# A two-by-two block product of seven instead of eight in the up projection of the second layer, with its down projection in groups of four

## The chip, the cores and the metric

The kernel runs on one core of one Trainium2 chip. The metric is the device time of one execution in microseconds (us). A core has five engines with instruction streams of their own, each worked off in order: TensorE (PE, with its weight loads shown as PEld), VectorE (DVE), ScalarE (ACT), GpSimd (POOL) and SyncE (SP), which here issues the transfers. A wait of an instruction holds up all that stands behind it on its engine.

## What is computed

The reference is one inference step of a two-layer backbone with D = 1024 over 128 context and 512 latent tokens. A layer has a mixer (two kinds of attention and a Fourier mixing), then a gated feed-forward part with a convolution of width three over the tokens. The change concerns the second layer's feed-forward part alone:

```python
h = _modulate(x_l, g_ffn_norm[l], sf, cf)
x_l = x_l + gf * _conv_ffn(h, w_up[l], w_conv[l], w_down[l])

def _conv_ffn(h, w_up_l, w_conv_l, w_down_l):
    u = h @ w_up_l                      # 1024 -> 2 * 2816
    up = jnp.pad(u, ((0, 0), (1, 1), (0, 0)))
    u = sum(up[:, j:j + N] * w_conv_l[j] for j in range(3))
    gate, val = jnp.split(u, 2, axis=-1)
    return (jax.nn.silu(gate) * val) @ w_down_l   # 2816 -> 1024
```

Context and latent tokens take their own modulation and the same weights. At the end comes a norm of both streams.

## The kernel before

Features lie on the partitions and tokens on the columns: 642 columns, of which two are spare, in two halves of 322 and 320. For the convolution each half is taken with a column more on either side, so an up product has 324 columns.

Products have nearly the precision of fp32. Every operand is split (`hi_lo`, L111 to L113): ScalarE copies it rounded to `hi`, and VectorE or GpSimd subtracts to get `lo`. `mm3` (L130 to L133) then issues three matmuls, hi by hi, hi by lo and lo by hi. A weight tile is loaded by a transfer into `raw` and split into `whi` and `wlo` (`weight`, L119 to L125); the feed-forward part has two tiles of each, and a third of its own (`weight3`, L898).

The feed-forward part (`ffn`, L888 to L1032) first does the output projection of the mixer in two passes, one for each half, 8 output tiles each, with residual and squares. After a pass `stats` (L221 to L241) makes the norm of that half and `modulate` (L244 to L262) writes the modulated tiles `hh`, `hl` for eight feature tiles.

Then come 22 tiles j of hidden features, in groups of 8, 8 and 6 (`FGROUPS`, L38). For each j, L972 to L988 take a gate tile and a value tile: a weight tile of 128x1024, and for each half of the columns 8 steps of the contraction by three matmuls, so 96 matmuls of 324 columns per j, in a PSUM bank per product. ScalarE makes the middle tap (L983), VectorE the outer two (L984, L986), straight from PSUM. ScalarE makes the silu (L989), GpSimd multiplies (L990), ScalarE casts to `gh`, and GpSimd subtracts for `gl` (L993). Behind each group, L1001 to L1029 do its share of the down projection: for each of eight output tiles m and each half three matmuls per j, then the residual on VectorE (L859), in two pieces for the first half and one for the second. The last group does so in two passes, one per half, each with squares, the norm, and the scaled output tiles `y` (L1025), sent by SyncE.

PSUM has six banks for these products. The order on each engine is set by a scheduler that simulates a timeline when the kernel is built; the code's order and the number of buffers bound it.

## Time and profile before

| what | value |
|---|---|
| times of three runs | 1838.87, 1839.2, 1846.52 us |
| median | 1839.2 us |
| span of the profiled execution | 1843.6 us |
| TensorE busy | 1717.2 us, 93% |
| VectorE busy | 1166.4 us, 63% |
| ScalarE busy | 779.4 us, 42% |
| GpSimd busy | 650.0 us, 35% |

The profile is of one execution, whose span is listed beside the times; all durations come from it. In it the second layer's up and down projections take from about 1345 us to 1828 us, and the end of the output about 16 us more. Busy time of TensorE's matmuls is modelled, and neighbours overlap in the rows: the pace of matmuls is read from their number in a stretch without waits.

### The profile page before, as it was taken

The numbers are of one execution on the slowest core, as the hardware profiler recorded it, in microseconds if no ns is written. First come the engines' busy times: TensorE is split into PE (matmuls) and PEld (weight loads), VectorE is DVE, ScalarE is ACT, GpSimd is POOL, SyncE is SP. The second block draws the span as 40 slices with busy tenths as digits, with TensorE's granted clock in tenths as the row PEclk, the third lists the DMA queues.
The fourth block names the chain that finished last, engine by engine and source line by source line (L and its number), as shares of the span: only waits on it lengthen the run. The fifth ranks groups of instructions, "written<-read, shape, count | busy, mean of one in ns | idle before, by whom it ended". The sixth has DMA issues, their size and how long they took to land. (4 is left out here: it accounts for less than half of the span.)

```text
span 1843.6 us, 29032 instructions
## 1 busy us (share of the span) xinstructions
PE 1717.2 (93%) x11160; PEld 1670.1 (91%) x11160; DVE 1166.4 (63%) x2051; ACT 779.4 (42%) x1494; POOL 650.0 (35%) x719
## 2 busy tenths in 40 slices
PE   6988899986999999999999798999999999999997
PEld 5878899876899999999998787998999999999997
DVE  7628765679799999734455388865544434443445
ACT  5436564643543123313343466765433313321332
POOL 6547454548422112201242576562212201220222
PEclk9889898988899999999999899999999999999998
DMA  7367654655255565322254576562312222222223
GB/s 279 96 210 208 193 172 149 207 175 171 82 182 172 183 202 164 111 73 73 63 169 135 177 214 183 176 205 73 103 35 74 76 72 78 70 81 69 78 69 118
DMA packets 81084, 249.70 MB, mean 135 GB/s; under 512 B 10417, under 2 KB 19761, under 8 KB 79281
## 3 DMA queue, kind: packets, MB, share of 16 engines
q1 hardware_dynamic: 74226, 209.13, 35.6%
q0 software_dynamic: 6720, 38.72, 7.6%
q8 instruction: 88, 1.44, 0.3%
q14 instruction: 50, 0.41, 0.1%
HBM read 203.43 MB, written 41.24 MB: 133 GB/s over the span
## 5 line engine op out<-in xcount | busy, mean ns | idle before, releaser
L132 PE MATMUL up<-hl_o,whi 128*128 128x324 f32 x1408 | 441.2, 314 | 2.7 <-POOL hl_o L113 2.7
L131 PE MATMUL up<-hh_o,whi 128*128 128x324 f32 x1408 | 440.4, 314 | 2.3 <-ACT hh_o L260 1.2
L133 PE MATMUL up<-hh_o,wlo 128*128 128x324 f32 x1408 | 440.8, 314 | 0.0
L112 ACT CAST whi<-raw 128x1024 fp32r<-128x1024 f32 (+2 forms) x210 | 207.0, 989 | 434.7 <-PE dn L132 204.7
L113 DVE TENSOR_TENSOR wlo<-raw,whi 128x1024 fp32r<-128x1024 f32 (+2 forms) x184 | 227.0, 1237 | 203.4 <-ACT whi L112 199.2
L990 POOL TENSOR_TENSOR cg<-cg,cv 128x644 f32<-128x644 f32 x44 | 73.2, 1664 | 665.4 <-DVE cv L986 653.9
L132 PEld LDWEIGHTS up<-hl_o,whi 128*128 128x128 f32 x1408 | 268.0, 190 | 4.4 <-POOL hl_o L113 4.3
L131 PEld LDWEIGHTS up<-hh_o,whi 128*128 128x128 f32 x1408 | 267.8, 191 | 3.0 <-ACT hh_o L112 1.6
L133 PEld LDWEIGHTS up<-hh_o,wlo 128*128 128x128 f32 x1408 | 267.1, 190 | 0.0
L131 PE MATMUL dn<-gh,whi 128*128 128x322 f32 x704 | 218.7, 314 | 5.0 <-ACT gh L112 3.9
L132 PE MATMUL dn<-gl,whi 128*128 128x322 f32 x704 | 220.1, 313 | 0.0
L133 PE MATMUL dn<-gh,wlo 128*128 128x322 f32 x704 | 218.9, 313 | 0.0
L149 DVE CUSTOM_DVE_ANT_0 junk<-ada,scond 128x1024 bf16<-128x1024 f32 x138 | 199.4, 1445 | 4.4 <-ACT scond L143 2.8
L477 DVE TENSOR_REDUCE nm<-sc 128x1 f32<-128x640 f32 (+1 forms) x180 | 126.5, 711 | 76.5 <-PE sc L576 56.2
L478 ACT ACTIVATE P<-sc,nm 128x640 f32<-128x640 f32 (+1 forms) x180 | 128.1, 713 | 74.9 <-DVE nm L477 56.6
L859 DVE SCALAR_TENSOR_TENSOR x_x<-dn,mods,x_x 128x128 f32<-128x128 f32 (+2 forms) x144 | 57.6, 436 | 132.8 <-PE dn L133 132.7
L131 PEld LDWEIGHTS dn<-gh,whi 128*128 128x128 f32 x704 | 133.4, 190 | 6.9 <-ACT gh L112 4.1
L133 PEld LDWEIGHTS dn<-gh,wlo 128*128 128x128 f32 x704 | 133.8, 190 | 0.4 <-DVE wlo L113 0.4
L132 PEld LDWEIGHTS dn<-gl,whi 128*128 128x128 f32 x704 | 133.9, 190 | 0.3 <-POOL gl L113 0.2
L131 PE MATMUL proj<-hh_n,whi 128*128 128x320 f32 (+1 forms) x320 | 109.0, 341 | 5.7 <-ACT whi L112 3.0
L133 PE MATMUL proj<-hh_n,wlo 128*128 128x320 f32 (+1 forms) x320 | 106.8, 334 | 0.0
L132 PE MATMUL proj<-hl_n,whi 128*128 128x320 f32 (+1 forms) x320 | 106.5, 333 | 0.0
(299 smaller groups left out, 3740.0 us busy)
## 6 DMA issues: line engine op xcount, KB each, us to landing
raw<-in_w_up SPq DMA_DIRECT2D x88, 512.0 KB, 3.6
...
```

The costliest lines, as they stand in the source:

```text
L112: nc.scalar.copy(out=hi, in_=src)
L113: (lo_eng or nc.vector).tensor_tensor(out=lo, in0=src, in1=hi.bitcast(F32), op=ALU.subtract)
L131: nc.tensor.matmul(out, lhsT=lh, rhs=rh, start=first, stop=False)
L132: nc.tensor.matmul(out, lhsT=lh, rhs=rl, start=False, stop=False)
L133: nc.tensor.matmul(out, lhsT=ll, rhs=rh, start=False, stop=last)
L149: nc.vector.tensor_tensor_reduce(out=junk, in0=wt, in1=scond[:, c], op0=ALU.mult, op1=ALU.add, scale=1.0, scalar=0.0, accum_out=mods[:, l, ...
L477: nc.vector.tensor_reduce(out=nm, in_=s_in, axis=ax, op=ALU.max, negate=True)
L478: nc.scalar.activation(out=p_out, in_=s_in, func=AF.Exp, bias=nm, scale=1.0, accum_out=s_out)
L859: nc.vector.scalar_tensor_tensor(out=x[:, o:o + w], in0=ps, scalar=gate, in1=x[:, o:o + w], op0=ALU.mult, op1=ALU.add)
L990: nc.gpsimd.tensor_tensor(out=c[0], in0=c[0], in1=c[1], op=ALU.mult)
```

## The change

In the second layer (`SEVEN`) a tile j's gate and value weights are seen as a two-by-two block matrix (gate and value by two halves of the contraction, each 128x512: wa, wb for the gate, wc, wd for the value), and the tokens as another (two halves of the contraction by two halves of the columns: b11, b12, b21, b22). Their product is made from seven block products, numbered in the code:

| product | weight | tokens | goes to |
|---|---|---|---|
| 1 | wa | b11 | bank A, copied to s1 |
| 2 | wb | b21 | bank A on top: gate, first half |
| 6 | x6 = wc + wd + wa | -(b22 - b12) - b11 | bank B; u2 = B + s1 |
| 7 | wc + wa | b22 - b12 | bank B on top; u3 = B + s1, then C + u3: value, second half |
| 4 | wd | (b22 - b12) + b11 - b21 | bank B on top; + s1: value, first half |
| 5 | x5 = wc + wd | b11 - b12 | bank C |
| 3 | wb + x6 | b22 | bank C on top; + u2: gate, second half |

The signs of the value tile are turned, and its convolution's weights with them. The token blocks are combined once, behind the norm (`modulate32` and the loop after it), in fp32, and split. The weight blocks are combined for each j by four additions on GpSimd. Each weight is split in pieces of 512 columns, two to a tile of the ring (`half_weight`). The up products of successive j are interleaved in an order written out by hand. Three of the four pairs of taps read an SBUF tile where all had read PSUM. The down projection goes in groups of 4, 4, 4, 4, 4 and 2, its weights loaded for two output tiles at a time, and `gh`, `gl` have 5 buffers, not 10.

```diff
-FGROUPS = ((0, 8), (8, 8), (16, 6))
+FGROUPS = (((0, 8), (8, 8), (16, 6)), ((0, 4), (4, 4), (8, 4), (12, 4), (16, 4), (20, 2)))
+SEVEN = (1,)
 ...
+    def modulate32(l, n, k, x, rb, h32, pool):
+        first = rb[0][0] == 0
+        for z in ((0, 130) if first else (644,)):
+            nc.gpsimd.memset(h32[:, z:z + 2], 0.0)
+        tt = pool.tile([P, HT], F32, name="nt", tag="t640")
+        for o, w, c, r in rb:
+            t = tt[:, o:o + w]
+            nc.vector.scalar_tensor_tensor(out=t, in0=x[:, o:o + w], scalar=gain[:, l, n, k, c:c + 1],
+                                           in1=r, op0=ALU.mult, op1=ALU.mult)
+            nc.scalar.activation(out=h32[:, o + 2:o + 2 + w], in_=t, func=AF.Identity,
+                                 bias=mods[:, l, 24 * n + k, c:c + 1], scale=1.0)
 ...
+            if seven:
+                nc.vector.tensor_scalar(out=wconv[:, :, 1, :], in0=wconv[:, :, 1, :], scalar1=-1.0, scalar2=None,
+                                        op0=ALU.mult)
 ...
-                    for k in range(NK):
-                        modulate(l, 1, k, xs[k], rb[hf], oh[k], ol[k], pool, MOD2_ENG[l][8 * hf + k] == "P")
+                    if not seven:
+                        for k in range(NK):
+                            modulate(l, 1, k, xs[k], rb[hf], oh[k], ol[k], pool, MOD2_ENG[l][8 * hf + k] == "P")
+                    elif hf == 0:
+                        for k in range(NK):
+                            modulate32(l, 1, k, xs[k], rb[0], h32[k], pool)
+                            hi_lo(oh[k][:, :324], ol[k][:, :324], h32[k][:, :324], on(MOD7[k]))
                 hh, hl = oh, ol
+            if seven:
 ...
+            if seven:
+                tp_ = fpx.enter_context(tc.tile_pool(name=f"ft{l}", bufs=1, side="left", reuse_waits="tile"))
+                th = [tp_.tile([P, 3, 324], F32R, name=f"th{k}") for k in range(4)]
+                tl = [tp_.tile([P, 3, 324], F32R, name=f"tl{k}") for k in range(4)]
+                for k in range(4):
+                    for i in (k, k + 4):
+                        modulate32(l, 1, i, xs[i], rb[1], h32[i], pool)
+                    b11, b12 = h32[k][:, 0:324], h32[k][:, 322:646]
+                    b21, b22 = h32[k + 4][:, 0:324], h32[k + 4][:, 322:646]
+                    ta = pool.tile([P, HT], F32, name="ta", tag="t640")
+                    tb = pool.tile([P, HT], F32, name="tb", tag="t640")
+                    nc.vector.tensor_tensor(out=ta[:, 324:], in0=b22, in1=b12, op=ALU.subtract)
+                    nc.vector.scalar_tensor_tensor(out=tb[:, :324], in0=ta[:, 324:], scalar=-1.0, in1=b11,
+                                                   op0=ALU.mult, op1=ALU.subtract)
+                    hi_lo(th[k][:, 1], tl[k][:, 1], tb[:, :324])
+                    nc.gpsimd.tensor_tensor(out=ta[:, :324], in0=b11, in1=b12, op=ALU.subtract)
+                    hi_lo(hh[k][:, 324:], hl[k][:, 324:], ta[:, :324], nc.gpsimd)
+                    nc.vector.scalar_tensor_tensor(out=tb[:, 324:], in0=tb[:, :324], scalar=-1.0, in1=b21,
+                                                   op0=ALU.mult, op1=ALU.subtract)
+                    hi_lo(th[k][:, 0], tl[k][:, 0], ta[:, 324:])
+                    hi_lo(hh[k + 4][:, 324:646], hl[k + 4][:, 324:646], h32[k + 4][:, 324:], nc.gpsimd)
+                    hi_lo(th[k][:, 2], tl[k][:, 2], tb[:, 324:])
+                hx.__exit__(None, None, None)
             gpl = fpx.enter_context(tc.tile_pool(name=f"fg{l}", bufs=1, side="left", reuse_waits="tile"))
             step = lambda n: None
             if l + 1 < L:
                 step = ada_list([(l, j) for j in range(40, 48)] + [(l + 1, j) for j in range(48)])
             acc = accs()
 ...
+            def rhs(n, k):
+                t, r = {1: (0, slice(0, 324)), 2: (4, slice(0, 324)), 3: (4, slice(322, 646)),
+                        5: (0, slice(324, 648))}.get(n, (None, {7: 0, 6: 1, 4: 2}.get(n)))
+                if t is None:
+                    return th[k][:, r], tl[k][:, r]
+                return hh[t + k][:, r], hl[t + k][:, r]
+            open_, turn3, gs_ = [], itertools.count(), {}
+            def half_weight(src):
+                n = src.shape[1]
+                if not open_:
+                    p = fp if next(turn3) % 3 == 2 else None
+                    t = [(p or gp).tile([P, 1024], F32R, name=nm, tag=nm, bufs=1 if p else 2) for nm in ("whi", "wlo")]
+                    open_.append(t)
+                    o = 0
+                else:
+                    t, o = open_.pop(), 512
+                hi, lo = (x[:, o:o + n] for x in t)
+                hi_lo(hi, lo, src)
+                return hi, lo
+            def down_weight(m, f0, nf):
+                if m % 2 == 0:
+                    raw = raw_tile((None, fp)[(f0 + nf + 1) % 2], 2).rearrange("p (m c) -> p m c", m=2)
+                    nc.sync.dma_start(out=raw[:, :, :128 * nf],
+                                      in_=A["w_down"][l, m:m + 2, :, 128 * f0:128 * (f0 + nf)].rearrange("m p c -> p m c"))
+                    gs_["raw"] = raw
+                return half_weight(gs_["raw"][:, m % 2, :128 * nf])
+            def seven_up(order):
+                st = {}
+                for j, n in order:
+                    if j not in st:
+                        d = st[j] = {}
+                        g, v = [raw_tile((None, fp)[j % 2], 2) for _ in range(2)]
+                        for gv, t in enumerate((g, v)):
+                            nc.sync.dma_start(out=t, in_=A["w_up"][l, j, gv])
+                        x = gpl.tile([P, 1024], F32, name="x12", tag="x12", bufs=2)
+                        wa, wb, wc, wd = g[:, :512], g[:, 512:], v[:, :512], v[:, 512:]
+                        d["w"] = {1: wa, 2: wb, 3: wb, 4: wd, 5: x[:, :512], 6: x[:, 512:], 7: wc}
+                        nc.gpsimd.tensor_tensor(out=x[:, :512], in0=wc, in1=wd, op=ALU.add)
+                        nc.gpsimd.tensor_tensor(out=x[:, 512:], in0=x[:, :512], in1=wa, op=ALU.add)
+                        nc.gpsimd.tensor_tensor(out=wc, in0=wc, in1=wa, op=ALU.add)
+                        d["s"] = pool.tile([P, HT], F32, name="s1u2", tag="t640")
+                        d["c"] = [ctile(0), ctile(1)]
+                    d = st[j]
+                    if n == 3:
+                        nc.gpsimd.tensor_tensor(out=d["w"][2], in0=d["w"][2], in1=d["w"][6], op=ALU.add)
+                    wh, wl = half_weight(d["w"][n])
+                    bank = {1: "A", 2: "A", 6: "B", 7: "B", 4: "B", 5: "C", 3: "C"}[n]
+                    if n in (1, 6, 5):
+                        d[bank] = pst("up")[:, :324]
+                    t = d[bank]
+                    for k in range(4):
+                        s = slice(128 * k, 128 * k + 128)
+                        mm3(t, wh[:, s], wl[:, s], *rhs(n, k), n in (1, 6, 5) and k == 0, k == 3, n not in (1, 6, 5))
+                    s1, u2 = d["s"][:, :324], d["s"][:, 324:]
+                    cw = wconv[:, j]
+                    if n == 1:
+                        nc.scalar.copy(out=s1, in_=t)
+                    elif n == 6:
+                        nc.vector.tensor_tensor(out=u2, in0=t, in1=s1, op=ALU.add)
+                    elif n == 2:
+                        taps(d["c"][0][:, 0], t, cw[:, 0])
+                    elif n == 7:
+                        u = pool.tile([P, HT], F32, name="u3c", tag="t640")
+                        nc.vector.tensor_tensor(out=u[:, :324], in0=t, in1=s1, op=ALU.add)
+                        nc.vector.tensor_tensor(out=u[:, 324:], in0=d["C"], in1=u[:, :324], op=ALU.add)
+                        taps(d["c"][1][:, 1], u[:, 324:], cw[:, 1])
+                    elif n == 4:
+                        d["v"] = pool.tile([P, HT], F32, name="cc", tag="t640")
+                        nc.vector.tensor_tensor(out=d["v"][:, :324], in0=t, in1=s1, op=ALU.add)
+                        taps(d["c"][1][:, 0], d["v"][:, :324], cw[:, 1])
+                    elif n == 3:
+                        nc.vector.tensor_tensor(out=d["v"][:, 324:], in0=t, in1=u2, op=ALU.add)
+                        taps(d["c"][0][:, 1], d["v"][:, 324:], cw[:, 0])
+                        st[j]["g"] = glu(d["c"])
+                    yield j, n, st[j].get("g") if n == 3 else None
+            if seven:
+                order = [(0, 1), (1, 1), (0, 2), (1, 2), (0, 6), (0, 5), (0, 7), (1, 6), (0, 4), (0, 3), (1, 5), (1, 7)]
+                for j in range(2, NFF):
+                    order += [(j, 1), (j, 6), (j - 1, 4), (j - 1, 3), (j, 5), (j, 2), (j, 7)]
+                order += [(NFF - 1, 4), (NFF - 1, 3)]
+                made = seven_up(order)
+                after = {j: (j + 1, 7) if j + 1 < NFF else (j, 3) for j in range(NFF)}
 ...
+                if seven:
+                    for j, n, g in made:
+                        if g:
+                            gs_[j] = g
+                        if (j, n) == after[f0 + nf - 1]:
+                            break
+                    G = [gs_.pop(j) for j in range(f0, f0 + nf)]
 ...
+GV7 = 5
+MOD7 = "VPVPVPVP"
+FB7 = {"nt": 4, "rb": 2, "sq": 2}
+TAG7 = {"ta": "nt", "tb": "sq", "s1u2": "nt", "u3c": "rb", "cc": "sq", "y": "nt"}
```

In numbers of instructions, an up tile j has 7 x 4 x 3 = 84 matmuls where it had 96, and TensorE has 264 fewer in all; the down matmuls are as many as before. Up to the end of the mixer the engines' orders are the same.

ScalarE where the second half's norm is ready: `nt` is the normed tile, `hh_o` the split tokens; before, it stood thus.

```order
L983 ACTIVATE cg<-up,wconv 128x322
L260 ACTIVATE hh_o_12601<-nt,mods 128x320
L260 ACTIVATE hh_o_12602<-nt,mods 128x320
L257 ACTIVATE nt<-nt,mods 128x320
L112 CAST hh_o_12603<-nt 128x320
L260 ACTIVATE hh_o_12604<-nt,mods 128x320
L260 ACTIVATE hh_o_12605<-nt,mods 128x320
L260 ACTIVATE hh_o_12606<-nt,mods 128x320
L257 ACTIVATE nt<-nt,mods 128x320
L260 ACTIVATE hh_o_12608<-nt,mods 128x320
L112 CAST hh_o_12607<-nt 128x320
L983 ACTIVATE cv<-up,wconv 128x322
```

After: `h_2` and the like are the fp32 tokens, `ta` and `tb` the combined blocks, `th` their split, `s1u` the copy of product 1.

```order
L116 CAST th_14229<-ta 128x324
L279 ACTIVATE h_3_13601<-nt,mods 128x320
L279 ACTIVATE h_7_13605<-nt,mods 128x320
L116 CAST hh_o_12608<-h_7_13605 128x322
L1126 COPY s1u_14344<-up 128x324
L1126 COPY s1u_14373<-up 128x324
L116 CAST th_14229<-tb 128x324
L116 CAST hh_o_12604<-ta 128x324
L116 CAST th_14230<-ta 128x324
L116 CAST th_14229<-tb 128x324
L116 CAST th_14230<-tb 128x324 x2
L116 CAST whi<-x_14340 128x512
```

The taps of the first up product stood ahead of the modulation; the two copies of s1 stand behind all eight modulations of the second half and 14 casts, and the first cast of x6's kind behind six more casts.

GpSimd within an up stretch, before, for two and more tiles j (`cg` and `cv` are the gate and value after the taps).

```order
L990 TENSOR_TENSOR cg<-cg,cv 128x644
L113 TENSOR_TENSOR gl<-cg,gh 128x644
L990 TENSOR_TENSOR cg<-cg,cv 128x644
L113 TENSOR_TENSOR gl<-cg,gh 128x644
L990 TENSOR_TENSOR cg<-cg,cv 128x644
L113 TENSOR_TENSOR gl<-cg,gh 128x644
```

After, in the same place (`x_17422` and the like hold x5 and x6 of a tile).

```order
L1037 TENSOR_TENSOR cg<-cg,cv 128x644
L1107 TENSOR_TENSOR x_17422<-raw 128x512
L1114 TENSOR_TENSOR raw<-raw,x_17277 128x512
L1108 TENSOR_TENSOR x_17422<-x_17422,raw 128x512
L1109 TENSOR_TENSOR raw<-raw 128x512
L117 TENSOR_TENSOR gl<-cg,gh 128x644
L1037 TENSOR_TENSOR cg<-cg,cv 128x644
L1114 TENSOR_TENSOR raw<-raw,x_17422 128x512
L117 TENSOR_TENSOR gl<-cg,gh 128x644
L1037 TENSOR_TENSOR cg<-cg,cv 128x644
L117 TENSOR_TENSOR gl<-cg,gh 128x644
```

Between multiplication and subtraction, which followed each other, four additions for a tile two further on now stand.

VectorE within an up stretch, before, a little over one tile j.

```order
L113 TENSOR_TENSOR wlo<-raw,whi 128x1024
L984 SCALAR_TENSOR_TENSOR cg<-up,wconv,cg 128x322
L986 SCALAR_TENSOR_TENSOR cg<-up,wconv,cg 128x322
L984 SCALAR_TENSOR_TENSOR cv<-up,wconv,cv 128x322
L986 SCALAR_TENSOR_TENSOR cv<-up,wconv,cv 128x322
L113 TENSOR_TENSOR wlo<-raw,whi 128x1024
L984 SCALAR_TENSOR_TENSOR cv<-up,wconv,cv 128x322
L986 SCALAR_TENSOR_TENSOR cv<-up,wconv,cv 128x322
L984 SCALAR_TENSOR_TENSOR cg<-up,wconv,cg 128x322
L986 SCALAR_TENSOR_TENSOR cg<-up,wconv,cg 128x322
```

After (`u3c` and `cc` are sums in SBUF, `s1u` holds s1 and u2).

```order
L1128 TENSOR_TENSOR s1u_15730<-up,s1u_15730 128x324
L117 TENSOR_TENSOR wlo<-raw,whi 128x512 x2
L1138 TENSOR_TENSOR cc<-up,s1u_15585 128x324
L1027 SCALAR_TENSOR_TENSOR cv<-cc,wconv,cv 128x322
L1141 TENSOR_TENSOR cc<-up,s1u_15585 128x324
L1029 SCALAR_TENSOR_TENSOR cv<-cc,wconv,cv 128x322
L117 TENSOR_TENSOR wlo<-raw,whi 128x512 x2
L1027 SCALAR_TENSOR_TENSOR cg<-cc,wconv,cg 128x322
L1029 SCALAR_TENSOR_TENSOR cg<-cc,wconv,cg 128x322
L117 TENSOR_TENSOR wlo<-raw,whi 128x512
L1027 SCALAR_TENSOR_TENSOR cg<-up,wconv,cg 128x322
L1133 TENSOR_TENSOR u3c<-up,s1u_15730 128x324
```

A subtraction for weights stood behind every four taps from PSUM; now weight subtractions, output additions and taps from SBUF alternate.

## Rows read from the trace of the kernel before

**Rows 1.** The page, part 1: span, then busy time, share and instructions by engine.

```profile
span 1843.6 us, 29032 instructions
PE 1717.2 (93%) x11160; PEld 1670.1 (91%) x11160; DVE 1166.4 (63%) x2051; ACT 779.4 (42%) x1494; POOL 650.0 (35%) x719
```

**Rows 2.** Five stretches: length, PE, PEld, DVE, ACT, POOL, clock, DMA share, GB/s.

```profile
1349.00:1353.50 4.50, 1.69 (x13) 1.44 (x13) 2.67 (x7) 0.73 (x2) 0.86 (x1) 0.86 0.00 0
1356.00:1359.00 3.00, 3.00 (x12) 3.00 (x12) 2.86 (x6) 1.95 (x5) 0.00 (x0) 0.50 0.00 0
1390.00:1780.00 390.00, 390.00 (x2623) 390.00 (x2622) 168.32 (x259) 119.85 (x170) 60.19 (x38) 1.00 0.24 73
1781.00:1828.00 47.00, 46.42 (x311) 45.24 (x309) 28.31 (x58) 19.13 (x31) 18.16 (x15) 1.00 0.41 121
1828.00:1843.60 15.60, 2.89 (x16) 2.62 (x16) 5.18 (x11) 0.47 (x1) 0.86 (x1) 0.57 0.24 85
```

**Rows 3.** Groups of instructions, 1390 to 1780 us: busy, mean ns | idle before.

```profile
L131 PE MATMUL up<-hh_o,whi 128*128 128x324 f32 x619 | 192.6, 311 | 0.0
...
L113 DVE TENSOR_TENSOR wlo<-raw,whi 128x1024 fp32r<-128x1024 f32 x53 | 65.0, 1226 | 109.6 <-ACT whi L112 109.6
...
L113 POOL TENSOR_TENSOR gl<-cg,gh 128x644 fp32r<-128x644 f32 x19 | 30.1, 1583 | 16.0 <-ACT gh L112 16.0
L986 DVE SCALAR_TENSOR_TENSOR cv<-up,wconv,cv 128x322 f32<-128x322 f32 x39 | 21.6, 553 | 1.4
...
L983 ACT ACTIVATE cv<-up,wconv 128x322 f32<-128x322 f32 x39 | 20.6, 527 | 42.3 <-PE up L133 42.3
...
L989 ACT ACTIVATE cg<-cg 128x644 f32<-128x644 f32 x20 | 14.6, 732 | 1.6 <-DVE cg L986 1.6
...
L859 DVE SCALAR_TENSOR_TENSOR x_x<-dn,mods,x_x 128x321 f32<-128x321 f32 x16 | 8.8, 551 | 35.0 <-PE dn L133 35.0
```

**Rows 4.** Timeline of the stretch's start: start us, duration us, instruction, [idle <-releaser].

```profile
1344.83 0.31 PE L131 MATMUL up<-hh_o,whi 128*128 128x324 f32 x1
...
1352.53 1.46 DVE L252 SCALAR_TENSOR_TENSOR nt<-x_x,gain,rsh 128x320 f32<-128x320 f32 x3 [1.01 <-PE rsh L237]
...
1353.72 0.91 PE L131 MATMUL up<-hh_o,whi 128*128 128x324 f32 x2 [1.23 <-ACT hh_o L260]
...
1355.15 0.75 POOL L113 TENSOR_TENSOR hl_o<-nt,hh_o 128x320 fp32r<-128x320 f32 x1 [4.22 <-ACT hh_o L112]
...
1359.65 0.31 PE L131 MATMUL up<-hh_o,whi 128*128 128x324 f32 x1
```

**Rows 5.** Timeline of the last tail: its first down matmul, and the last output tiles.

```profile
1781.22 0.31 PE L131 MATMUL dn<-gh,whi 128*128 128x322 f32 x1
...
1833.79 1.47 DVE L1025 SCALAR_TENSOR_TENSOR y<-x_x,c_g_fin,rsh 128x321 f32<-128x321 f32 x3 [1.63 <-PE rsh L237]
...
1839.76 1.07 DVE L1025 SCALAR_TENSOR_TENSOR y<-x_x,c_g_fin,rsh 128x321 f32<-128x321 f32 x2 [1.09 <-DMA out_yl<-y]
```

**Rows 6.** Groups of instructions of other widths, 1200 to 1843.6 us.

```profile
L113 DVE TENSOR_TENSOR wlo<-raw,whi 128x768 fp32r<-128x768 f32 x16 | 15.1, 956 | 9.3 <-ACT whi L112 9.0
...
L113 DVE TENSOR_TENSOR tl<-tp,th 128x512 fp32r<-128x512 f32 x22 | 15.0, 684 | 6.8 <-ACT th L112 6.7
...
L112 ACT CAST th<-tp 128x512 fp32r<-128x512 f32 x22 | 12.9, 588 | 8.8 <-PE tp L530 8.7
```

**Rows 7.** A 512-wide group of GpSimd, 560 to 1000 us.

```profile
L353 POOL TENSOR_TENSOR rb<-x,c_cos 128x512 f32<-128x512 f32 x2 | 2.3, 1150 | 20.7 <-ACT x L336 20.7
```

**Rows 8.** Timeline at three places where GpSimd and VectorE work together.

```profile
554.74 1.74 POOL L113 TENSOR_TENSOR gl<-cg,gh 128x644 fp32r<-128x644 f32 x1 [0.84 <-ACT gh L112]
...
554.98 2.59 DVE L113 TENSOR_TENSOR wlo<-raw,whi 128x1024 fp32r<-128x1024 f32 x1
...
1324.61 1.53 POOL L216 TENSOR_TENSOR acc_x<-acc_x,sq 128x320 f32<-128x320 f32 x1 [2.81 <-ACT sq L214]
...
1399.19 1.59 POOL L990 TENSOR_TENSOR cg<-cg,cv 128x644 f32<-128x644 f32 x1 [10.28 <-DVE cv L986]
...
1399.99 0.55 DVE L984 SCALAR_TENSOR_TENSOR cg<-up,wconv,cg 128x322 f32<-128x322 f32 x1 [0.94 <-ACT cg L983]
```

101 lines of the change are left out of this document (60 added, 41 removed).

## The prediction

> **What bounds the kernel now.** I read the page's busy shares first, then the same by stretches, then the groups of the second layer's feed-forward stretch, and last single rows at its two ends. TensorE is busy 93% of a span of 1843.6 us [rows 1]. In the 390 us of up and down projections it is busy every moment at a granted clock of 1.00, while VectorE works 168, ScalarE 120 and GpSimd 60 us of them [rows 2]: TensorE alone sets that stretch. Its price is read there: 390 us / 2623 matmuls = 0.1487 us each. The mean of 311 ns [rows 3] is no price, since neighbours overlap. At the ends this is not so. When the last output projection is done, TensorE runs the 24 up matmuls of the half whose norm is ready, then waits for the other half's norm, and comes back at a granted clock of 0.50, 12 matmuls in 3 us, or 0.25 to 0.27 us each [rows 2, 4]. The end is the second tail: last matmul, residual, norm, eight output tiles [rows 5].
>
> The profiled execution's span is 4.4 us over the median of the three times, 1839.2 us. I count changes against the span and put them on the median. A measurement of this kernel can tell about 0.5%, 9.2 us, from no change.
>
> **Removed.** Per feature tile j, eight block products are seven: 8 × 12 = 96 matmuls become 84. Over 22 tiles that is 264 fewer, all of 324 columns in a stretch where TensorE never waits: 264 × 0.1487 = **−39.2 us**, if the stretch stays TensorE's. The Trainium skill ("TensorE: Matmul & The Clock Gate", "Wait — 56ns, not 53.3ns?") gives columns by 2.4 GHz plus some 2.5 ns, 137.5 ns here; by that the term would be 36.3 us. The row has the higher price and decides.
>
> **Added per tile j.** Weights are split in 512-wide pieces, seven per j. VectorE takes 1.226 us for 1024 columns and 0.956 for 768 [rows 3, 6], so 1.05 ns a column and 0.69 us for 512; a 512-wide subtraction elsewhere took 0.684 [rows 6]. Seven make 4.8 us where two made 2.45. Five output additions (one PSUM operand or more, 324 wide) are like a tap, 0.55 [rows 3]: 2.8 us. Eight taps stay, 4.4 us. VectorE per j: 2.45 + 4.4 = 6.9 before, **12.0** after, of which TensorE's 84 × 0.1487 = 12.5 leave it 0.5 to spare in an up stretch. ScalarE: seven casts at 0.59 [rows 6], four taps at 0.53, the copy of s1 like a tap, silu and the cast gh 0.73 each [rows 3]: 8.2, no bound. GpSimd: before 2 × 1.58 = 3.2 [rows 3]; four 512-wide additions at 1.15 [rows 7] come on top: 7.8, no bound by itself.
>
> But two of these engines disturb each other. A GpSimd subtraction at 554.74 and a VectorE subtraction of two SBUF tiles at 554.98 overlap; the latter took 2.59 us and ends 1.09 after GpSimd's, its time alone being 1.226 [rows 3, 8]. At 1399.19 GpSimd multiplies for 1.59 while VectorE's tap from PSUM takes its usual 0.55 [rows 8]. So what blocks is two SBUF operands on VectorE. The Trainium skill ("SBUF — State Buffer", "SBUF: two separate sides") calls this a lock held for a whole instruction and names just that condition; the rows agree, and by that rule the whole of the overlap would be lost, the slower rival below.
>
> After the change three of the four tap pairs read SBUF tiles and not PSUM, and seven subtractions read two SBUF tiles: 4.8 + 6 × 0.55 = 8.1 us per j on VectorE that block against GpSimd, 65% of 12.5. In a group of four the up stretch is 50 us of TensorE, the down stretch 192 × 0.1487 = 28.6. GpSimd has 4 × 7.8 = 31 us; the additions of two tiles (9.2) can run in the down stretch, since the raw buffers hold two tiles ahead. So 22 us fall in the up stretch, and 65% of it, 14, lands on VectorE's blocked work. VectorE has 48 us there; 48 + 14 = 62 against 50. The weight ring, four products of 1.8 us, lends about 7. Not all blocked time is lost, since VectorE also waits for products; I take about 10 of the 14, which leaves 50 − 48 − 10 + 7 = −1, and a stall brings back the half clock for some matmuls (0.27 against 0.149 [rows 2, 4]), so 3 us per group. Five groups: **+15 us**. Ends: +4 (nothing but group starts) and +36 (all 14 lost: 62 − 50 − 7 = 5, plus 2 for the clock, five times).
>
> The down matmuls are as many as before. The two residuals of the first half and the one of the second are done per tile and group, so six groups, not three, add 3 × 8 × 3 = 72 VectorE operations of at most 0.55 [rows 3]; a down stretch then holds 8 × (3 × 0.55 + 0.69) = 19 us of VectorE beside TensorE's 28.6: hidden. Weight DMA stays at 73 GB/s against 121 in the tail [rows 2]: hidden.
>
> **The start of the stretch.** Before: the first up matmul starts at 1344.83; the 48th would start 47 × 0.1487 later, at 1351.8, and starts at 1359.65 [rows 4]: 7.8 us are lost. After: two products of 12 can run ahead as before. The next two (n = 2) add into the same banks, so they wait for ScalarE's copies of s1, which stand behind eight modulations and 14 casts of the second half. VectorE has to do 19 operations of 0.55 before the last of these modulations, 10.5 us and about 4 of blocking by GpSimd's 12 operations beside it: 1352.5 [rows 4] + 14.5 = 1367. The 24 matmuls of n = 2 then take until about 1374 at half clock. Product n = 6 needs x6 = x5 + wa, which GpSimd makes after 12 operations of 0.75 to 1.53 (free, and beside VectorE [rows 4, 8]) and as the third of three additions of 1.15: 1353.5 + 9 to 18 + 3.5 = 1366 to 1375; then a cast, and the subtraction behind 32 operations of VectorE, 1352.5 + 16 + 4 to 8 = 1373 to 1377. So TensorE is in full work at about 1377 with 48 matmuls done, 25 us behind the pace in place of 7.8: **+17 us**. Ends: +9 (no blocking, copies 4 us earlier by another order of casts) and +22 (all blocking at its upper ends).
>
> **The tail.** Before, from the first matmul of the last down projection at 1781.22 to the end are 62.4 us, of which 288 × 0.1487 = 42.8 are matmuls: 19.6 lost [rows 5]. After, the last group is two tiles, 96 matmuls, 14.3 us. The last tile's chain (output addition, taps, silu, product on GpSimd, gh, gl: 0.55 + 0.53 + 1.1 + 0.73 + 1.58 + 0.73 + 1.58, about 7) ran beside matmuls of five finished tiles; now one is finished, whose matmuls for the six free banks are 18, 2.7 us: 4 more. Each m has 6 matmuls of a half, 0.9 us, and VectorE's weight split of 256 columns (0.42 by the line of the two wider ones) and two residual pieces (under 0.55 each) go beside them at about 1.2: 2 more over eight m. The output tiles of the first half, hidden before by the second pass, now end behind the last residuals, in the wait for the norm, 0 to 3. Sum **+6 us**, from +3 to +10.
>
> **Sum.** −39.2 + 17 + 15 + 6 = −1.2: 1839.2 − 1.2 = **1838 us**.
>
> **The rivals.** *Faster, the shared access stalls nothing:* if the ring and VectorE's own waits take up the blocking, steady +3, start +12 and tail +3 remain: −21, **1818 us**. For it speaks that TensorE has no wait at all in 390 us now and the ring is as long in time; against it, that VectorE goes from 43% of that stretch to 12.0 of every 12.5 us. *Slower, VectorE is the pace of the up stretches:* all 14 us blocked per group are lost, +36, with +17 and +6 for the ends: +20, **1859 us**. It decides where blocked time passes 50 − 48 + 7 = 9 us a group. For it speaks the 2.59 of [rows 8], where nearly the whole overlap was lost; against it, that GpSimd's additions have two tiles of room and the scheduler may place them where VectorE reads PSUM. *The change does not do what it says:* matmuls are not fewer in time, for example since TensorE must reload or wait in the same bank; then the three additions stand alone and the time is 1877. The order has 264 matmuls fewer, so this has little.
>
> **How the numbers follow.** Forecast 0.42, faster 0.31, slower 0.25, not as it says 0.02. Range: the forecast with its terms' ends gives 1839 − 39 + 9 + 4 + 3 = 1816 to 1839 − 39 + 22 + 36 + 10 = 1868; all terms at one end together are unlikely, so 1818 to 1860, which takes in both rivals' times. Faster than 1830: 0.31; within 0.5%: 0.42; slower than 1848.4: 0.27.
>
> **What would show it.** Removed: the pace in a down stretch stays 0.149 and TensorE's matmuls are 264 fewer. Start: the gap in TensorE's rows after the first 24 up matmuls, ended by the s1 copy and then by x12, near 25 us in all. Steady: in an up stretch TensorE waits on the subtraction wlo, VectorE's share is near 95%, and wlo takes over 0.69 on average; a mean of 0.7 would make the faster rival right. Tail: last group's first matmul to the end, near 40 us. The forecast is wrong if the up stretches show no wait, or a pace over 14 us per j.

## The result, and the profile after

The changed kernel takes 1872.31 us (median of four runs, 1870.33 to 1874.08) against 1839.71 for the kernel before on the same chips: a ratio of 1.0172, 95% interval 1.015 to 1.0194. It is 32.6 us slower, where 1838 and a range to 1860 were forecast.

The page's head of the changed kernel: span, then busy time, share and instructions by engine, to be read beside [rows 1].

```profile
span 1868.1 us, 29191 instructions
PE 1695.0 (91%) x10896; PEld 1638.6 (88%) x10896; DVE 1370.1 (73%) x2376; ACT 835.9 (45%) x1674; POOL 792.4 (42%) x795
```

There are 264 fewer matmuls, as the order said. VectorE works 204 us more and GpSimd 142, and TensorE's share falls. The same by stretches (length, PE, PEld, DVE, ACT, POOL, clock, DMA share, GB/s): two of the start, one up and one down stretch of a group.

```profile
1350.00:1360.00 10.00, 0.00 (x0) 0.00 (x0) 10.00 (x17) 7.27 (x18) 7.38 (x9) 0.50 0.00 0
1360.00:1370.00 10.00, 5.70 (x24) 5.43 (x24) 10.00 (x10) 3.87 (x10) 9.42 (x8) 0.67 0.00 1
1469.00:1525.00 56.00, 53.02 (x340) 51.70 (x339) 52.12 (x71) 27.33 (x52) 30.64 (x19) 0.97 0.19 63
1525.00:1554.30 29.30, 28.77 (x193) 28.27 (x192) 20.79 (x42) 7.69 (x13) 7.02 (x5) 1.00 0.35 97
```

Where [rows 2] had a TensorE without a gap and VectorE at 43%, VectorE is now busy every moment of the start and 93% of an up stretch, with GpSimd at half of it, and TensorE waits.

To see how much is lost where, I count from the first up matmul, since the orders are the same up to there: it starts at 1344.83 before and at 1339.86 after, a difference in which the change has no part. From there to the end are 498.8 us before and 528.3 after, **29.5 more**, against 32.6 in the medians. Every run below but the last is one execution: three of the kernel before lie between 1838.87 and 1846.52 us, and in the fourteen traces the first up matmul starts anywhere from 1336.9 to 1346.3, so small differences are read from the traces and not from the times. In a stretch, the time from its first matmul's start to its last one's, less 0.1487 us for each matmul between, is what TensorE lost there. A time between two stretches goes to the later one. All kernels of this study, in us:

| kernel | first 72 up matmuls | rest of the first up stretch | later up stretches | down, but the last | last down | behind the last matmul | first up to end |
|---|---|---|---|---|---|---|---|
| before | 7.9 | 0.3 | 0.5 | -0.5 | 3.7 | 16.0 | 498.8 |
| changed | 31.1 | 10.0 | 21.6 | 7.0 | 9.1 | 17.8 | 528.3 |
| no additions | 17.1 | 0.9 | 0.6 | 1.0 | 9.1 | 16.9 | 477.2 |
| idle additions | 17.1 | 21.0 | 21.1 | 4.5 | 9.4 | 16.7 | 521.5 |
| all taps from PSUM | 30.1 | 11.8 | 29.2 | -0.4 | 8.5 | 17.4 | 528.2 |
| groups only | 6.8 | 0.1 | 0.7 | 1.2 | 9.4 | 18.5 | 507.7 |
| constant additions | 33.6 | 4.9 | 15.0 | 19.5 | 9.9 | 19.0 | 533.6 |
| fills | 26.2 | -0.1 | 0.6 | 1.6 | 10.3 | 17.4 | 487.8 |
| early start | 21.8 | 9.3 | 23.0 | 6.4 | 9.4 | 24.7 | 526.2 |
| mixed, early | 18.7 | 8.7 | 11.2 | 11.9 | 8.9 | 24.6 | 515.6 |
| VectorE's additions | 25.4 | 3.5 | 0.5 | 18.9 | 9.3 | 16.7 | 506.0 |
| mixed, end mended | 19.3 | 9.2 | 7.1 | 11.9 | 8.0 | 17.2 | 504.4 |
| VectorE's, end mended | 16.1 | 8.6 | -0.4 | 16.0 | 8.4 | 16.8 | 497.2 |
| whole tile | 16.1 | 7.9 | 4.1 | 1.0 | 7.8 | 17.6 | 486.1 |

Matmuls cost 3168 x 0.1487 = 471.1 us before and 39.2 less with seven products. So the 29.5 are -39.2 + 23.2 (start) + 9.8 (rest of the first up stretch) + 21.1 (later up stretches) + 7.5 (down) + 7.2 (last down and end), within rounding.

The start, in TensorE's waits (start us, duration, instruction, [idle before, and what ended it]):

```profile
1361.19 0.64 PE L136 MATMUL up<-hh_o,whi 128*128 128x324 f32 x1 [13.70 <-ACT s1u L1126]
1372.06 0.64 PE L136 MATMUL up<-th,whi 128*128 128x324 f32 x1 [5.17 <-ACT whi L116]
1376.22 0.64 PE L138 MATMUL up<-hh_o,wlo 128*128 128x324 f32 x1 [2.71 <-DVE wlo L117]
...
1413.80 0.64 PE L136 MATMUL up<-th,whi 128*128 128x324 f32 x1 [6.61 <-ACT whi L116]
```

First the copies of s1, as forecast; then the cast of x6, then a subtraction; and once more, 40 us later, the cast of an x6. By then the sum x6 was there (GpSimd's last addition of that kind had ended at 1410.7, and the cast began at 1413.15): the cast stood on ScalarE behind a silu that waited for VectorE's tap.

```profile
1412.50 0.74 ACT L1036 ACTIVATE cg<-cg 128x644 f32<-128x644 f32 x1 [2.96 <-DVE cg L1029]
```

What VectorE and GpSimd did around that time (x2 and x3 are rows of two and three operations):

```profile
1363.28 3.05 POOL L1107 TENSOR_TENSOR x<-raw 128x512 f32<-128x512 f32 x2
1366.30 1.52 POOL L1108 TENSOR_TENSOR x<-x,raw 128x512 f32<-128x512 f32 x1
...
1363.60 1.57 DVE L1014 SCALAR_TENSOR_TENSOR tb<-tb,h 128x324 f32<-128x324 f32 x1
1365.09 1.60 DVE L1009 SCALAR_TENSOR_TENSOR tb<-ta,h 128x324 f32<-128x324 f32 x1
1366.61 1.55 DVE L117 TENSOR_TENSOR tl<-tb,th 128x324 fp32r<-128x324 f32 x1
...
1371.04 4.52 DVE L117 TENSOR_TENSOR tl<-tb,th 128x324 fp32r<-128x324 f32 x3
```

The two go in lockstep: one addition, one VectorE operation, about 1.5 us for each pair. The subtraction of 324 columns took 0.48 us at 1362.10 in the same trace. For the 12 us of eight additions VectorE is held to the pace of GpSimd.

In the groups (stretch 1440 to 1780 us; count, busy, mean ns), beside [rows 3]:

```profile
L117 DVE TENSOR_TENSOR wlo<-raw,whi 128x512 fp32r<-128x512 f32 x111 | 109.0, 998 | 12.7 <-ACT whi L116 12.6
...
L1037 POOL TENSOR_TENSOR cg<-cg,cv 128x644 f32<-128x644 f32 x16 | 28.0, 1752 | 85.4 <-ACT cg L1036 85.4
...
L1109 POOL TENSOR_TENSOR raw<-raw 128x512 f32<-128x512 f32 x16 | 25.2, 1574 | 0.0
...
L1107 POOL TENSOR_TENSOR x<-raw 128x512 f32<-128x512 f32 x16 | 22.0, 1374 | 91.8 <-DMA raw<-in_w_up 91.8
...
L1029 DVE SCALAR_TENSOR_TENSOR cv<-u3c,wconv,cv 128x322 f32<-128x322 f32 x16 | 20.1, 1257 | 0.4
...
L1029 DVE SCALAR_TENSOR_TENSOR cg<-up,wconv,cg 128x322 f32<-128x322 f32 x16 | 8.7, 546 | 0.1
```

Subtractions of 0.69 take 1.00. Of the six taps from SBUF the slowest takes 1.26, two more 0.93 and 0.88, and three 0.55, as do the taps from PSUM. The four additions, expected at 1.15 by [rows 7], take 1.37 to 1.57. What TensorE waits for most in the groups is the sum u3 of product 7, which VectorE must read before product 4 adds to the bank (us in total, times, longest):

```profile
PE up L136 <- DVE u3c L1133: 8.5, 8, 1.8
```

### The profile page after: what moved, and what is told of

It reads as the page before. It is cut to its first block, busy times and chain, and to the rows that moved or that the text cites. A ratio compares the mean times of both kernels' runs of the same rounds, so it can differ in the third digit from the quotient of the medians.

```text
span 1868.1 us, 29191 instructions
## 1 busy us (share of the span) xinstructions
PE 1695.0 (91%) x10896; PEld 1638.6 (88%) x10896; DVE 1370.1 (73%) x2376; ACT 835.9 (45%) x1674; POOL 792.4 (42%) x795
## 5 line engine op out<-in xcount | busy, mean ns | idle before, releaser
L116 ACT CAST whi<-raw 128x512 fp32r<-128x512 f32 (+3 forms) x300 | 224.7, 767 | 382.1 <-PE dn L137 185.3
L117 DVE TENSOR_TENSOR wlo<-raw,whi 128x512 fp32r<-128x512 f32 (+3 forms) x274 | 285.9, 1056 | 87.0 <-ACT whi L116 81.4
L136 PE MATMUL up<-hh_o,whi 128*128 128x324 f32 x1056 | 334.3, 318 | 16.8 <-ACT s1u L1126 13.7
L137 PE MATMUL up<-hl_o,whi 128*128 128x324 f32 x1056 | 334.5, 317 | 2.7 <-POOL hl_o L117 2.7
L138 PE MATMUL up<-hh_o,wlo 128*128 128x324 f32 x1056 | 333.1, 317 | 3.4 <-DVE wlo L117 3.4
L1037 POOL TENSOR_TENSOR cg<-cg,cv 128x644 f32<-128x644 f32 x44 | 77.2, 1754 | 448.1 <-DVE cv L1029 316.9
L136 PEld LDWEIGHTS up<-hh_o,whi 128*128 128x128 f32 x1056 | 204.2, 194 | 18.6 <-ACT s1u L1126 13.8
L137 PEld LDWEIGHTS up<-hl_o,whi 128*128 128x128 f32 x1056 | 204.0, 193 | 4.4 <-POOL hl_o L117 4.3
L138 PEld LDWEIGHTS up<-hh_o,wlo 128*128 128x128 f32 x1056 | 203.1, 193 | 4.6 <-DVE wlo L117 4.6
L877 DVE SCALAR_TENSOR_TENSOR x_x<-dn,mods,x_x 128x128 f32<-128x128 f32 (+2 forms) x216 | 86.0, 434 | 91.4 <-PE dn L138 90.9
```

The source lines that it names most:

```text
L116: nc.scalar.copy(out=hi, in_=src)
L117: (lo_eng or nc.vector).tensor_tensor(out=lo, in0=src, in1=hi.bitcast(F32), op=ALU.subtract)
L136: nc.tensor.matmul(out, lhsT=lh, rhs=rh, start=first, stop=False, skip_group_check=more)
L137: nc.tensor.matmul(out, lhsT=lh, rhs=rl, start=False, stop=False, skip_group_check=more)
L138: nc.tensor.matmul(out, lhsT=ll, rhs=rh, start=False, stop=last, skip_group_check=more)
L877: nc.vector.scalar_tensor_tensor(out=x[:, o:o + w], in0=ps, scalar=gate, in1=x[:, o:o + w], op0=ALU.mult, op1=ALU.add)
```

## The experiments

### Without the additions

```diff
-                        d["w"] = {1: wa, 2: wb, 3: wb, 4: wd, 5: x[:, :512], 6: x[:, 512:], 7: wc}
-                        nc.gpsimd.tensor_tensor(out=x[:, :512], in0=wc, in1=wd, op=ALU.add)
-                        nc.gpsimd.tensor_tensor(out=x[:, 512:], in0=x[:, :512], in1=wa, op=ALU.add)
-                        nc.gpsimd.tensor_tensor(out=wc, in0=wc, in1=wa, op=ALU.add)
...
-                        nc.gpsimd.tensor_tensor(out=d["w"][2], in0=d["w"][2], in1=d["w"][6], op=ALU.add)
...
+                        d["w"] = {1: wa, 2: wb, 3: wb, 4: wd, 5: wd, 6: wc, 7: wc}
```

> The changed kernel without GpSimd's four additions of weights per tile j: products 3, 5, 6 read raw blocks in place of the sums, so the weights of those products are not the reference's; all matmuls, casts, subtractions, output additions and taps stay. Theory (GpSimd's additions and VectorE's two-SBUF operations shut each other out): the 31 us lost in the first 72 up matmuls fall to about 20, the 9.6 us lost later in the first group and the 21.5 us in the later up stretches nearly vanish (under 6 in sum); time about 1838. Rival (the chain of weights is only long: GpSimd, then ScalarE, then VectorE): the same, since the chain's first link is gone. A third reading (VectorE's own number of operations, 12 us per tile against 12.5, is enough to stall): under 10 us gained, time 1862 or more.

1820.55 us beside 1842.28 for the kernel before. The full up stretches behind the first lose nothing at all, the first 72 matmuls 17.1. The third reading is out: VectorE's own number of operations fits. In an up stretch it is busy 43.5 of 49.9 us, and TensorE always:

```profile
1447.20:1497.10 49.90, 49.90 (x338) 49.90 (x337) 43.45 (x73) 28.08 (x52) 10.39 (x6) 1.00 0.23 70
```

The down stretch behind it, and the subtractions of this run:

```profile
1497.10:1525.80 28.70, 28.70 (x194) 28.50 (x193) 18.53 (x40) 7.25 (x12) 3.18 (x2) 1.00 0.33 101
```

```profile
L117 DVE TENSOR_TENSOR wlo<-raw,whi 128x512 fp32r<-128x512 f32 x138 | 103.9, 778 | 16.3 <-ACT whi L116 15.7
```

So VectorE is busy 62.0 us in an up and a down stretch together; in the changed kernel's four full groups it is 71.8 in the mean, 9.8 more. At 0.78 the subtractions are above 0.69 even here, where GpSimd has only its products and subtractions for the gate.

All 51 us from 528.3 to 477.2 hang on GpSimd's four additions per tile; by which way, this run doesn't say. At the start it can't be set beside the changed kernel: without sums to wait for, products on `th` come ahead of product 2 there, and so they do in the next run.

### Additions that nobody reads

```diff
+                        d["w"] = {1: wa, 2: wb, 3: wb, 4: wd, 5: wd, 6: wc, 7: wc}
                         nc.gpsimd.tensor_tensor(out=x[:, :512], in0=wc, in1=wd, op=ALU.add)
                         nc.gpsimd.tensor_tensor(out=x[:, 512:], in0=x[:, :512], in1=wa, op=ALU.add)
-                        nc.gpsimd.tensor_tensor(out=wc, in0=wc, in1=wa, op=ALU.add)
+                        nc.gpsimd.tensor_tensor(out=x[:, :512], in0=wc, in1=wa, op=ALU.add)
```

> As the run without additions, but GpSimd makes all four additions per tile j into a scratch tile that nobody reads: the products' weights are raw blocks, not the reference's. Theory (they shut each other out on the way to SBUF): the up stretches lose nearly what the changed kernel loses, 15 us or more after the first 72 matmuls, and VectorE's 512-wide subtractions take 1.0 us or more in the mean; time 1858 to 1872. Rival (only the chain through GpSimd is long): as without additions, about 1838, subtractions at 0.7.

1860.25 us: 44 of the 51 us are back though nobody waits for an addition. The subtractions are at 1.03 us, and from 1400 us on TensorE waits (us in total, times, longest) mostly for VectorE:

```profile
PE up L136 <- DVE u3c L1134: 11.5, 9, 2.3
PE up L138 <- DVE wlo L117: 7.2, 6, 3.1
```

The long chain from GpSimd to TensorE is not needed for the loss. What it leaves, beside the blocking, is that an addition holds a raw tile and waits for one.

### All taps from PSUM

```diff
-                        nc.vector.tensor_tensor(out=d["v"][:, :324], in0=t, in1=s1, op=ALU.add)
-                        taps(d["c"][1][:, 0], d["v"][:, :324], cw[:, 1])
+                        nc.vector.tensor_tensor(out=t, in0=t, in1=s1, op=ALU.add)
+                        taps(d["c"][1][:, 0], t, cw[:, 1])
```

and so for products 3 and 7, the latter into a bank of its own.

> The changed kernel with the output sums of products 4, 3 and 7 written into PSUM banks, so that all taps read PSUM again as before the change; nothing else differs, the result is the same. Theory (VectorE is blocked where both its operands are in SBUF): blocked work of VectorE per tile j falls from 8.1 to 4.8 us, taps take 0.55 again, and of the 31 us lost in up stretches behind the first 72 matmuls a half goes, 10 to 20 us; time 1852 to 1862. Rival (the chain through GpSimd): within 5 us of 1872. A loss from banks held longer would show as waits of TensorE for taps.

1872.16 us and 528.2 from the first up matmul, as in the changed kernel: a miss. The taps did take 0.55 us:

```profile
L1029 DVE SCALAR_TENSOR_TENSOR cv<-u,wconv,cv 128x322 f32<-128x322 f32 x16 | 8.8, 552 | 0.6
```

yet TensorE loses as much, and waits longer than in the changed kernel for the operation that must read product 7's bank before product 4 adds to it:

```profile
PE up L136 <- DVE u3c L1133: 26.0, 14, 2.7
```

The subtractions stay at 1.00 us. VectorE is down to 49.0 of 57.6 us of an up stretch, and waits itself: at 1508.73 it idles 1.84 us for the cast of an x6 behind a GpSimd addition. So with the blocking of the taps gone, the chain through GpSimd or the bank taken for the sum holds as much; the run doesn't tell which, and it stays open. Taking off a half of the blocked work is not worth a half of the loss.

### Groups of four alone

```diff
-SEVEN = (1,)
+SEVEN = ()
```

> One part of the change alone: the second layer with eight products as before, but its down projection in six groups of four, four, four, four, four and two. Theory (grouping costs little beside the rest): 3 to 9 us over the kernel before, 1843 to 1849, nearly all in the last group; no loss in the up stretches. Rival (short groups are what costs: each change between up and down stalls): 20 us or more over, 1860, with a loss at each change of stretch.

1849.07 us beside 1842.28, 8.9 us more from the first up matmul, of which 8.2 stand in the last down stretch and behind it, and 1.8 in the other down stretches; the first up stretch loses 1.2 less. The rival is out. In the tail TensorE waits mostly once, for the last tile's cast:

```profile
PE dn L136 <- ACT gh L116: 3.1, 1, 3.1
```

In the changed kernel the same wait is 3.79 us, at 1834.19.

### Additions of constants, and fills in their place

The changed kernel's additions with other operands, and then each one replaced by two fills of the same tile, which read nothing:

```diff
-                        nc.gpsimd.tensor_tensor(out=x[:, :512], in0=wc, in1=wd, op=ALU.add)
+                        nc.gpsimd.tensor_tensor(out=x[:, :512], in0=hh[4][:, :512].bitcast(F32), in1=hh[5][:, :512].bitcast(F32), op=ALU.add)
```

> GpSimd makes four 512-wide additions per tile j as in the changed kernel, but of two constant tiles in SBUF, into the tile that products 5 and 6 take as weights; products 7 and 3 take raw blocks. So the weights of products 3, 5, 6 and 7 are not the reference's; no addition waits for a transfer or holds a raw tile. Theory (an addition that reads SBUF shuts VectorE's two-SBUF operations out): losses in the later up stretches as in the changed kernel, 4 to 7 us a group, weight subtractions near 1.0 us; time 1850 to 1868. Rival (the additions wait for transfers and hold raw tiles, which delays the next): no loss in up stretches, subtractions near 0.77, about 1825.

```diff
-                        nc.gpsimd.tensor_tensor(out=x[:, :512], in0=wc, in1=wd, op=ALU.add)
+                        nc.gpsimd.memset(x[:, :512], 0.0)
+                        nc.gpsimd.memset(x[:, :512], 0.0)
```

> As the run with additions of constants, with each addition replaced by two 512-wide fills of the same tile: GpSimd has work at the same places with the same releases and readers, but reads nothing from SBUF. Weights of products 3, 5, 6 and 7 are not the reference's. Theory (the reads shut VectorE out): up stretches lose under 1 us a group, weight subtractions 0.70 to 0.80, time 1820 to 1832. Rival (GpSimd's time delays its own products for the gate, or the chain from GpSimd to TensorE is what costs): as with additions of constants, 1850 or more.

1879.14 against 1834.16 us, on the same chip. The losses of the constant additions lie 3.5 us to an up and 4.5 to a down stretch, more in the down stretches than I expected; the fills lose 2.2 us in all of them, up and down. One up stretch of each:

```profile
1474.20:1527.70 53.50, 51.15 (x338) 49.85 (x337) 49.64 (x65) 24.80 (x46) 31.08 (x21) 1.00 0.21 66
```

```profile
1459.30:1509.00 49.70, 49.70 (x337) 49.70 (x336) 42.81 (x72) 28.15 (x52) 23.11 (x36) 1.00 0.21 71
```

The subtractions of weights in the first and in the second:

```profile
L117 DVE TENSOR_TENSOR wlo<-raw,whi 128x512 fp32r<-128x512 f32 x111 | 113.7, 1039 | 12.4 <-ACT whi L116 12.3
```

```profile
L117 DVE TENSOR_TENSOR wlo<-raw,whi 128x512 fp32r<-128x512 f32 x120 | 86.7, 739 | 18.8 <-ACT whi L116 18.6
...
L1118 POOL MEMSET x<- 128x512 f32 x15 | 8.0, 532 | 0.0
```

GpSimd's eight fills per tile take 4.2 us, four additions would take 4.6 by [rows 7]; no raw tile is held in either kernel, and the readers are the same. What differs is that the additions read SBUF; a fill is also another and shorter instruction, and no run parts the two. But VectorE's taps from PSUM kept 0.55 us beside the additions, which points to the way to SBUF. For the groups this settles the way: 34.5 us are lost behind the first up stretch, ahead of the last down stretch, with additions of constants, and 2.2 with fills. The Trainium skill ("SBUF — State Buffer", "SBUF: two separate sides") names a lock between a VectorE operation with two SBUF inputs and a GpSimd operation that reads SBUF; both runs agree with that condition.

### An early start

The first two tiles' additions, product 1 and the copy of s1 are written ahead of the second half's modulation:

```diff
+                made = seven_up(order)
+                next(made), next(made)
             if seven:
                 tp_ = fpx.enter_context(tc.tile_pool(name=f"ft{l}", bufs=1, side="left", reuse_waits="tile"))
```

with x5 and x6 in a pool of their own, s1 and the output tiles in a ring of two.

> The changed kernel with the first two tiles' weight additions, their first products and the copies of s1 written ahead of the second half's modulation (s1 in a ring of its own, x5 and x6 in a space that is free earlier); the result is the same. Theory (the start loses 31 us because copies stand behind the modulation on ScalarE, and because eight additions run beside VectorE's combinations): the 48th up matmul comes 8 us or more sooner, the loss of the first 72 falls from 31 to 15 to 23 us, time 1856 to 1866. Rival (VectorE's 32 operations alone set the start, wherever the rest stands): the loss stays within 4 us of 31.

1868.7 us. The 48th up matmul comes with a loss of 1.4 in place of 19.7, the first 72 lose 21.8 in place of 31.1: copies and additions did stand where the prediction said, and 10.0 us of the first up stretch are won. The time is 2.7 us over what I expected since 6.9 us are lost at the end: output tiles had four buffers and now had two, and wait for their transfers.

```profile
1855.73 1.08 DVE L1202 SCALAR_TENSOR_TENSOR y<-x_x,c_g_fin,rsh 128x321 f32<-128x321 f32 x2 [1.59 <-DMA out_yl<-y]
```

That was my edit's doing, and no property of the start.

### Additions divided between the engines

On top of the early start, x5 and x6 on VectorE, the other two on GpSimd, sums of products 4 and 3 in their banks:

```diff
-                        nc.gpsimd.tensor_tensor(out=x[:, :512], in0=wc, in1=wd, op=ALU.add)
-                        nc.gpsimd.tensor_tensor(out=x[:, 512:], in0=x[:, :512], in1=wa, op=ALU.add)
+                        nc.vector.tensor_tensor(out=x[:, :512], in0=wc, in1=wd, op=ALU.add)
+                        nc.vector.tensor_tensor(out=x[:, 512:], in0=x[:, :512], in1=wa, op=ALU.add)
```

> The run with the early start, and besides the additions for x5 and x6 on VectorE, those for products 7 and 3 on GpSimd, and the sums of products 4 and 3 written into their PSUM banks; the result is the same. Theory: GpSimd's part of blocking halves (about 3 us a group back), VectorE gets 1.4 us a tile more, so that the up stretches stay VectorE's; later groups lose 4 to 8 us as before, the start 12 to 20: 1850 to 1864. Rival (the chain through GpSimd is what costs in up stretches): 2 us a group or less, about 1840.

1859.82 us. A later group (its up and its down stretch) loses 5.1 us instead of the 6.6 of the early start, so 1.5 came back where I expected about 3. The two parts of the edit were made at once, and their shares stay open.

### All additions on VectorE

```diff
-                        nc.gpsimd.tensor_tensor(out=wc, in0=wc, in1=wa, op=ALU.add)
+                        nc.vector.tensor_tensor(out=wc, in0=wc, in1=wa, op=ALU.add)
```

and so for all four, and nothing else in the changed kernel.

> The changed kernel with all four weight additions of a tile on VectorE and none on GpSimd; the result is the same. Theory (a GpSimd addition that reads SBUF holds VectorE up for nearly as long as VectorE would need for it, 0.69 us): VectorE per tile 12.0 + 2.8 = 14.8 us against 12.5 of matmuls, so up stretches lose 6 to 10 us a group, near the 7 lost with GpSimd; the start is shorter by 4 to 8, since eight additions take 5.5 us and not 12 of both engines; time 1862 to 1876. Rival (GpSimd's additions cost VectorE much less than their own time): 1885 or more.

1854.16 us, 8 us under the lower end of what I expected, and 22.3 less from the first up matmul than the changed kernel. One up and one down stretch, and two groups:

```profile
1469.90:1519.60 49.70, 49.70 (x337) 49.70 (x336) 47.52 (x80) 26.09 (x49) 10.17 (x6) 1.00 0.21 71
1519.60:1551.10 31.50, 29.56 (x195) 28.58 (x194) 24.18 (x49) 9.24 (x17) 3.15 (x2) 1.00 0.31 92
```

```profile
L117 DVE TENSOR_TENSOR wlo<-raw,whi 128x512 fp32r<-128x512 f32 x117 | 95.3, 828 | 5.4 <-ACT whi L116 5.2
...
L1108 DVE TENSOR_TENSOR x<-x,raw 128x512 f32<-128x512 f32 x16 | 11.0, 685 | 0.3
```

The up stretches lose nothing, with VectorE at 96%: what doesn't fit goes to the start of the down stretch, 2.9 us each. Both theories were off. From the first up matmul the 88 additions cost 28.8 us over the run without them if VectorE makes them, and 51.1 if GpSimd does. My step was to think VectorE's up stretch a bound by itself; over a group it has the down stretch too. And VectorE's busy time is not what sets the two apart: in an up and a down stretch together it is 71.8 us in either kernel, yet 2.8 us a group are lost here and 6.7 there. What makes the rest (GpSimd's longer way to its sums, or the places at which VectorE is held) no run shows.

### Put together

The same with the early start, the sums of products 4 and 3 in PSUM, four buffers for output tiles and last groups of three and three; first with mixed additions, then with all on VectorE.

```diff
-(12, 4), (16, 4), (20, 2))
+(12, 4), (16, 3), (19, 3))
```

> The run with the early start and mixed additions, with four buffers for the output tiles as in the changed kernel, and the last two groups of three and three tiles in place of four and two; the result is the same. Theory: the wait behind the last matmul falls from 24.6 to 17 or 18 us, the last group loses 2 us less, all else as there: 9 us less than that run, 6 to 12 us over the kernel before. Rival (the output tiles' buffers are not what made the end longer): the end stays at 24.

> The same with all four additions on VectorE. Theory: VectorE, at 93% in the up stretches of the mixed run, takes 1.4 us a tile more and is held up less by as much; within 6 us of the mixed run. Rival: each addition moved from GpSimd to VectorE costs its full 0.69 us: 1.4 x 22 = 30 us slower.

1845.1 and 1843.13 us beside 1843.34 for the kernel before. The end is back at 17 us in both. From the first up matmul the mixed kernel needs 504.4 us, 5.6 more than before and just under what was expected, and the other 497.2: 7.1 less, so here too an addition is cheaper on VectorE. Seven products are then level with eight, as far as one execution of each can tell. What is left lies at the start of the down stretches, 2.5 to 4.3 us each.

The last run puts the change to the down projection later, behind all seven products of the tile that follows the group:

```diff
-                    order += [(j, 1), (j, 6), (j - 1, 4), (j - 1, 3), (j, 5), (j, 2), (j, 7)]
+                    order += [(j, 1), (j, 6)]
+                    if j - 1 not in ends:
+                        order += [(j - 1, 4), (j - 1, 3)]
+                    order += [(j, 5), (j, 7), (j, 2), (j, 4), (j, 3)] if j in ends else [(j, 5), (j, 2), (j, 7)]
...
-                after = {j: (j + 1, 7) if j + 1 < NFF else (j, 3) for j in range(NFF)}
+                after = {j: (min(j + 1, NFF - 1), 3) for j in range(NFF)}
```

> The run with all additions on VectorE, early start and groups of 4, 4, 4, 4, 3 and 3, and besides the tile behind each group is finished (its seven products) ahead of the group's down projection, so that five products, 8.9 us, instead of three, 5.3 us, stand between the last product of the group and its down matmuls; the result is the same. Theory (what is left of losses between groups, 2.5 to 4.3 us at each start of a down stretch, is the chain from the last product over taps, silu, product and split to TensorE): these fall under 1 us, 8 to 12 us in all, and the kernel is 0.3 to 0.7% faster than the kernel before. Rival (VectorE's work is the bound over a whole group, wherever the change is put): the losses move into the up stretches, within 3 us of the run without it, level with the kernel before.

1833.39 us (median of six) beside 1840.99: a ratio of 0.9955, interval 0.9938 to 0.9973. It beats both kernels, the one before by 7.6 us. The down stretches but the last lose 1.0 us in all in place of 16.0, and 4.4 came into the up stretches. An up stretch between two changes, and a down stretch:

```profile
1454.00:1501.60 47.60, 46.38 (x313) 46.14 (x312) 41.14 (x71) 23.14 (x44) 6.72 (x4) 1.00 0.22 69
1507.80:1534.00 26.20, 26.20 (x178) 26.09 (x176) 22.59 (x47) 8.44 (x14) 4.74 (x3) 1.00 0.21 61
```

Of the 39.2 us that seven products take away, this trace keeps 12.7 from the first up matmul on; it is of the fastest of the six executions, 1826.43 us, and by the medians 7.6 are kept. The first up stretch takes 15.8 (24.0 against 8.1 before), the last down stretch and the end 5.7.

## Why the prediction was wrong

The forecast's sum had four terms.

**Removed, -39.2: right.** In every stretch without waits the pace stayed at 0.1487: the four full up stretches without additions lose 0.1 us or less each.

**Start, +17, measured +23.2: right up to where the forecast ended, too small behind it, and over its upper end of 22.** The chain was the right one: copies of s1, then x6. The 49th matmul starts at 1372.06, which is 25.1 us behind the pace, and 17.2 more than the 7.9 of the kernel before, as forecast. But TensorE was not "in full work" from there on. The next 23 matmuls lost 6.0 us more, 2.71 of them in the wait for the subtraction at 1376.22, most of the rest at the lower of the two clocks (0.27 us a matmul; granted clock 0.50 from 1376.3 to 1380). The forecast had the eight additions as something to wait for, and not as something that runs beside VectorE: three subtractions of 0.48 ahead of that one took 4.52. With fills, in the same order of products, the 49th matmul is 23.7 behind and the 72nd 26.2, so the reads of GpSimd's additions make about 5 of the 31.1. The wait for s1 is as long with fills, the wait for x6's cast shorter:

```profile
1366.07 0.64 PE L136 MATMUL up<-hh_o,whi 128*128 128x324 f32 x1 [13.70 <-ACT s1u L1131]
1375.48 0.64 PE L136 MATMUL up<-th,whi 128*128 128x324 f32 x1 [3.57 <-ACT whi L116]
```

**Groups, +15, measured 9.8 + 21.1 + 7.5 = 38.4: the failed step.** The work was well counted. VectorE's 71.8 us in an up and a down stretch, less 10.4 of residuals, are 61.3 for the up products, where the forecast had 48 + 14 = 62; without the additions they are 51.6. Of the 61.3 the down stretch took 10.7, where the forecast let the weight ring lend 7; 50.6 were left for an up stretch in which TensorE needs 50.0. It took 55.1 all the same. What failed is the step "Not all blocked time is lost, since VectorE also waits for products; I take about 10 of the 14". Without additions VectorE idles 6.4 us of an up stretch at no cost to TensorE; with them it still idled 4.5, so waits took up 1.9 us of blocked time and not 4, and TensorE waited for VectorE where it was held. A full group lost 6.7 us, 5.2 in its up and 1.5 in its down stretch, where the forecast had 3 and the slower rival 7. That the rival's sum with all 14 lost, 5 us an up stretch, meets the 5.2 is in part luck, since it has neither the idle 4.5 nor the 10.7.

So the slower rival came true for the groups: it said +36 (five times 7 is 35), and 1859 in all, since its start was too short as well. Not seen at all were the 9.8 us of the rest of the first up stretch, with the 6.61 us wait for an x6's cast behind a blocked tap, and the 7.5 of the down stretches, into which work of the up stretches spills; the forecast had called VectorE's work there hidden.

**Tail, +6, measured +7.2: right**, and as forecast from groups of four alone, whose run has +8.2.

With the measured terms the sum is -39.2 + 23.2 + 38.4 + 7.2 = 29.6, and the time 1869, against 1872.3 measured; the 3 us between are the difference of the medians from the profiled executions and have no cause shown here. The rival that GpSimd does not disturb is out. That blocking decides beyond about 9 us a group was not tested: the run with all additions on VectorE has as much work on that engine and loses less than half as much. The row of the blocked subtraction [rows 8] had shown nearly the whole overlap lost, and the forecast counted it so; it went softer in what VectorE's waits would take up.
